# A two-layer hybrid decoder trunk on one core: another order of the DRAM round trips on GpSimd's queue

## The chip, the core and the metric

The kernel runs on one core of a Trainium2 chip. The metric is the device time of one execution in microseconds; where several runs are given, their median. The profile is one execution, recorded by the hardware profiler. Engine names are those of the profile: PE is TensorE's matrix multiply and PEld its weight load, DVE is VectorE, ACT is ScalarE, POOL is GpSimd, SP is SyncE. A DMA that GpSimd issues stands in GpSimd's own instruction queue, between its other instructions.

## What is computed

Two layers over 256 tokens of width 1024, batch 1, in float32. Each layer, shortened from the reference:

```python
h = rms_norm(x, norm_g[l])
q_a, k_a, v_a, q_h, f_h, i_h, q_m, z = split(h @ w_in[l])      # 7 x 512 columns, and 1536 for the gate z
o_a = moba_attention(rope(rms_norm(q_a)), rope(rms_norm(k_a)), v_a)   # 8 heads of 64, causal over the one block
o_h = rms_norm(hgrn2_chunkwise(q_h, f_h, i_h, lb[l]), o_norm)         # 4 heads of 128, gated linear recurrence
k_m, v_m = split(rms_norm(mem, mem_norm_g[l]) @ w_mem_kv[l])
o_m = memory_attention(rms_norm(q_m), rms_norm(k_m), v_m)             # 4 heads of 128 over 256 memory tokens
y = concatenate([o_a, o_h, o_m]) * silu(z)
x = x + y @ w_out[l]
```

With 256 tokens and blocks of 256 keys there is no fully past block, so the block-sparse attention reduces to causal attention.

## The kernel before

**Weights.** Every weight passes through in chunks of 512 KB: `wr` is the chunk as loaded by SyncE's queue (4 buffers), `wh` its rounded high part, cast on ScalarE (lines 186 and 189; 3 buffers), `wl` the rest, formed on VectorE (lines 198 and 201; 3 buffers). A product takes three matmul passes, high by high, high by low and low by high, into four PSUM accumulators `acc`. Chunks are loaded up to five ahead, `wh` up to three and `wl` up to two ahead of TensorE.

**Order of one layer.** Memory keys and values; the projections f_h, q_h, k_a, i_h, q_a, the gate of the recurrent group (`zh`), q_m, v_a; then the gates of the other two groups, eight chunks c0 to c7 of the kind `acc<-hT,wh` and `acc<-hT,wl`; then `w_out`, twelve chunks (line 1164), which start with the four of the recurrent group. Of each gate chunk the low half of the accumulator is copied out by ScalarE (`al`, line 323) and added by VectorE (`as`, line 324).

**Side work.** Around this main row of matmuls run generators, small programs that yield between their pieces: `g_hgrn` (the recurrence), `g_moba` with two units `g_moba_unit` (four heads each), `g_mem_unit` and so on. A generator's piece is written into the program between two main matmul groups, and the framework's scheduler then places each instruction on its engine from a simulated timeline and the dependences. On an engine, instructions run strictly in the order so placed.

**The round trips.** `across` (lines 88 to 110) turns a tile over partitions and columns: VectorE transposes 32x32 blocks into `blk`, one DMA stores `blk` to a DRAM tile `there`, and four DMAs load it back, each of them a quarter of the destination, 32 partitions. The four loads need the store's landing. Keys use SyncE's queue; three trips per layer use GpSimd's:

- the softmax P of unit 0 of the first group, to `PT` (768 KB)
- the P of unit 1, to `PT` (768 KB)
- the recurrent group's gated output `zh` (512 KB, line 754, `y_turned`). After it ScalarE casts it to `yh` (line 125, two instructions) and VectorE forms `yl` (line 126); these are the left-hand sides of the first four chunks of `w_out`.

Between them on GpSimd stand the small powers `hgr` and `qmr` (line 600) and `nrm` (line 1059), which the memory group's exponentials need. In `y_turned`, the generator waits, while the program is written, until unit 1's P has been transposed (`turned1`).

**What stands around w_out.** Between the first `w_out` matmuls stand the `PT` matmuls of the two units (line 244 and 240, `sd<-PT,va`) and the memory group's (`sd<-mP,vmh`); before them, in chunk c6, the transposes of the memory group's softmax (line 1128, `sd<-ident,P`).

Of the kernel before, what the change touches and what calls it, by code (L numbers as in the profile page):

```python
# [3 lines left out]

# [41 lines left out]
def hymba_kernel(ctx: ExitStack, tc: tile.TileContext, x, mem, mem_t, positions, w_in, w_out, w_mem_kv,  # L46
                 gains, moba_g, out):
    nc = tc.nc
# [15 lines left out]
    def room(what, n=1):  # L64
        while held[what] + n > room_of[what]:
            yield

    def take(*whats):
        for w in whats:
            yield from room(w)  # L70
        while any(held[w] >= room_of[w] for w in whats):
            yield
        for w in whats:
            held[w] += 1

    def side_tile():
        held["sd"] += 1
        assert held["sd"] <= 4
        return psum.tile([128, 512], F32, name="sd", tag="sd", bufs=4)

    def rel(what="sd", n=1):
        held[what] -= n

    def small(name, n):
        return sb.tile([128, n], F32, name=name, tag=name, bufs=2)


    def across(dst, src, n, stage=None, free=None, name=None, q=None):
        q = q or nc.sync
        if stage is None:  # L90
            yield from room("blk")
            held["blk"] += 1
        tag = stage or "blk"
        blk = sb.tile([128, 4, n * 32], F32, name="blk", tag=tag, bufs=1)
        nc.vector.transpose(blk.rearrange("p c (n i) -> p c n i", n=n),
                            src.rearrange("p (n c i) -> p c n i", n=n, c=4))
        if free is not None:
            rel(free)
        if name is not None:
            done.add(name)  # L100
        yield 2
        there = away.tile([4, 32, 4, n * 32], F32, name="there", tag="there", bufs=2)
        q.dma_start(there.rearrange("q j c r -> (q j) c r"), blk)
        if stage is None:
            rel("blk")
        yield 4
        for c in range(4):
            q.dma_start(dst[c * 32:c * 32 + 32], there[:, :, c].rearrange("q j r -> j q r"))  # L108
            if c == 1:
                yield  # L110

    def turned(a, stage=None, q=None):
        yield from across(a.rearrange("p (q r) -> p q r", q=4), a, 8, stage, q=q)
        yield 5

    def strips(a):
# [5 lines left out]
    def unstripped(oh, ol, a):  # L122
        for t in range(2):
            src, to = strips(a)[:, :, t], strip_of(oh, t)
            nc.scalar.copy(to, src)  # L125
            nc.vector.tensor_tensor(strip_of(ol, t), src, to.bitcast(F32), op=OP.subtract)
# [82 lines left out]
    done = set()  # L209
    T = {}  # L210
# [28 lines left out]
    def mm(o, a, b, s, e):  # L239
        nc.tensor.matmul(o, lhsT=a, rhs=b, start=s, stop=e)  # L240
# [337 lines left out]
    zh = sb.tile([128, 2, 512], F32, name="zh")  # L578
# [24 lines left out]
    def g_km(l, acc):  # L603
# [25 lines left out]
        kml = kt.bitcast(F32R)  # L629
        g = gkq[:, l:l + 1]  # L630
        yield from across(kt.rearrange("p (q r) -> p q r", q=4), kn.rearrange("p t s -> p (t s)"), 8)
        while f"ih{l}" not in done:
            yield
# [103 lines left out]
    def y_tiles(br):  # L737
        if f"y{br}" not in T:
            T[f"y{br}"] = [sb.tile([128, 4, 256], F32R, name=f"y{c}{br}", tag=f"y{c}{br}", bufs=1) for c in "hl"]
        return T[f"y{br}"]  # L740

    def y_store(l, br, u, po):
        yh, yl = (a.rearrange("p k s -> p (k s)")[:, u * 512:(u + 1) * 512] for a in y_tiles(br))
        ys = sb.tile([128, 512], F32, name="ys", tag="sq", bufs=2)
        nc.vector.tensor_tensor(ys, po, zT[br][:, u * 512:(u + 1) * 512], op=OP.mult)
        nc.scalar.copy(yh, ys)
        nc.vector.tensor_tensor(yl, ys, yh.bitcast(F32), op=OP.subtract)
        rel()
        for k in (2 * u, 2 * u + 1):
            done.add(f"y{4 * br + k}_{l}")  # L750

    def y_turned(l):
        flat = zh.rearrange("p t s -> p (t s)")
        while f"turned1{l}" not in done:
            yield
        yield from turned(flat, "hq0", nc.gpsimd)
        unstripped(*y_tiles(H_), flat)
        yield
        for k in range(4):
            done.add(f"y{4 * H_ + k}_{l}")  # L760

    def g_hgrn(l):
# [121 lines left out]
        for t in range(2):  # L884
# [5 lines left out]
            rel()  # L890
            yield
        yield from y_turned(l)


    def g_qk(l, q, acc):
# [37 lines left out]
        if q == 0:  # L933
            o = o.rearrange("p (h s) -> p h s", h=4)
            for t in range(2):
                yield from room("sd")
                pt = side_tile()
                for p in range(4):
                    nc.tensor.transpose(pt[:, p * 128:(p + 1) * 128], kr[:, t, p * 128:(p + 1) * 128], ident)  # L939
                nc.scalar.copy(o[:, :, t * 128:(t + 1) * 128], heads(pt, 4))  # L940
                rel()
                yield
        else:
            yield from across(o.rearrange("p (q r) -> p q r", q=4), flat, 8)
            yield 5
# [13 lines left out]
    def second(u):  # L959
        qT, kT = T["qT"], T["kT"]  # L960
        ps = [side_tile() for _ in range(2)]
        for pi in range(2):
            for e in range(2):
                mm_row(ps[e][:, pi * 256:(pi + 1) * 256].rearrange("p (t q i) -> p t q i", t=2, q=4),
                       qT[64 * e:64 * e + 64, 2 * u + pi, 128:256], strips(kT)[64 * e:64 * e + 64, 2 * u + pi])
        return ps

    def second_masked(u, ps, P, mx):
        for i in range(4):
            pi, e = divmod(i, 2)  # L970
            masked(P, i, 1, ps[e][:, pi * 256:(pi + 1) * 256], mx)
        rel("sd", 2)

    def g_moba_unit(l, u, P, mx):
        rq, nr = T["rq"], T["nr"]
        nb = small("nba%d" % u, 8)
        sm = small("sma%d" % u, 8)
        ri = small("ria%d" % u, 8)
        if u:
            yield from room("sd", 2)  # L980
            ps = second(u)
            yield
            second_masked(u, ps, P, mx)
        nc.vector.tensor_tensor(nb.rearrange("p (t h) -> p t h", t=2), mx.rearrange("p (t h) -> p t h", t=2),  # L984
                                nr.rearrange("p (t h) -> p t h", t=2)[:, :, 4 * u:4 * u + 4], op=OP.mult)
        yield
        for t in range(2):
            for i in range(4):
                c, r = t * 4 + i, t * 8 + 4 * u + i
                nc.scalar.activation(P[:, i, kc[t]], P[:, i, kc[t]], AF.Exp, bias=nb[:, c:c + 1],  # L990
                                     scale=rq[:, r:r + 1], accum_out=sm[:, c:c + 1])
            yield
        yield
        nc.vector.reciprocal(ri, sm)
        for t in range(2):
            for i in range(4):
                c = t * 4 + i
                nc.vector.tensor_scalar(P[:, i, kc[t]], P[:, i, kc[t]], ri[:, c:c + 1], None, op0=OP.mult)
        yield 2
        tag = ("PTh", "PTl")[u]  # L1000
        yield from take(tag)
        PT = sb.tile([128, 4, 384], F32, name="PT", tag=tag, bufs=1)
        yield from across(PT, P.rearrange("p i s -> p (i s)"), 12, free="P", name=f"turned{u}{l}", q=nc.gpsimd)
        yield 13
        while f"va{l}" not in done or f"z{A_}{l}" not in done:
            yield
        va = T["va"]
        yield from room("sd")
        po = side_tile()
        for i in range(4):  # L1010
            h = 4 * u + i
            rows, c = slice(64 * (i % 2), 64 * (i % 2) + 64), (i // 2) * 256
            pieces = PT.rearrange("p q (n s) -> p n q s", n=12)[:, 3 * i:3 * i + 3]
            o = po[rows, c:c + 256].rearrange("p (b q s) -> p b q s", b=2, q=4)
            (mm if i else mm_row)(o, va[:, 0, h * 64:(h + 1) * 64], pieces[:, 0:2], True, False)
            mm(o[:, 1], va[:, 1, h * 64:(h + 1) * 64], pieces[:, 2], False, True)
        rel(tag)
        yield
        y_store(l, A_, u, po)
# [258 lines left out]
```

## Time and profile before

| | us |
|---|---|
| median of three runs (396.27 to 397.12) | 396.33 |
| the profiled execution | 399.69 |
| its span, first to last instruction | 397.9 |
| PE busy | 390.5 |
| DVE busy | 314.6 |
| ACT busy | 251.1 |
| POOL busy | 70.3 |

The sums of the prediction are made against the profiled execution. Its span is 1.8 us shorter than its own time, and its time is 3.36 us above the median of the runs. Times in the profile's rows count from the span's start. A row of the timeline gives start, duration, engine, line, operation and shape; x4 means four instructions merged; the brackets say how long the engine had been idle before and what ended the idle time. A PE row's duration holds the time in the pipeline; in an undisturbed row of 128x512 matmuls one starts every 0.23 us or so. Layer 0's and layer 1's instructions are the same but for a few set-up steps.

### The profile page before, as it was taken

To read this page: it belongs to the slowest core of one execution; us is meant where nothing else is said; L and a number is where in the kernel's file an instruction comes from. 1 tells how busy PE (TensorE), PEld (TensorE's weight loads), DVE (VectorE), ACT (ScalarE), POOL (GpSimd) and SP (SyncE) were. 2 spreads that over 40 slices of the span, in tenths; PEclk is the share of its full clock that TensorE was granted. 3 is DMA by queue.
4 is the path that set the end of the run, shared out by engine and by line. 5 is a ranking of instruction groups with operands and counts; after the bars stand their busy time and mean duration, and the time that the engine had idled before them with its cause. 6 is when DMAs were issued, how large, how long until landed. Compare 5 with 4: busy or idle time off the path is not lost.

```text
span 397.9 us, 7596 instructions
## 1 busy us (share of the span) xinstructions
PE 390.5 (98%) x2871; PEld 326.1 (82%) x2871; DVE 314.6 (79%) x606; ACT 251.1 (63%) x422; POOL 70.3 (18%) x109
## 2 busy tenths in 40 slices
PE   8999999999999999999999999999999999979996
PEld 5888888878788888788888888887888789867885
DVE  4789999889759998964576889799965999766743
ACT  5998746557778669544466766546856884954440
POOL 2013401604103432000000040050330061400000
PEclk9999999999999999999999999999999999999999
DMA  8986794377634989546565469637943398981612
GB/s 267 411 294 213 245 244 158 100 259 218 202 110 152 238 308 263 205 122 219 188 202 169 164 215 238 234 107 226 249 163 107 105 281 271 270 236 55 203 61 105
DMA packets 24901, 80.33 MB, mean 202 GB/s; under 512 B 3233, under 2 KB 5665, under 8 KB 24865
## 3 DMA queue, kind: packets, MB, share of 16 engines
q1 hardware_dynamic: 22304, 71.31, 56.0%
q0 software_dynamic: 2272, 8.39, 7.9%
q8 instruction: 22, 0.36, 0.4%
q10 hardware_dynamic: 288, 0.15, 0.1%
q14 instruction: 15, 0.11, 0.1%
HBM read 72.51 MB, written 7.34 MB: 201 GB/s over the span
## 4 chain that ended last, share of the span: by engine, by line
PE 86%; DMA 4%; DVE 4%; POOL 2%; issue 2%; ACT 1%; SPq 0%; ACTq 0%; DVEq 0%; POOLq 0%
PE acc L240 58%; PE acc L1164 17%; PE sd L240 5%; PE sd L244 3%; DMA zh<-there 3%; DMA wr<-in_w_mem_kv_dram 1%; DVE wl L198 1%; PE sd L453 1%; ACT wh L186 1%; POOL rka L904 1%; POOL PT L108 0%; PE sd L1068 0%; PE sd L939 0%; PE sd L1128 0%; POOL rtB L548 0%
## 5 line engine op out<-in xcount | busy, mean ns | idle before, releaser
L198 DVE TENSOR_TENSOR wl<-wr,wh 128x1024 fp32r<-128x1024 f32 x96 | 116.8, 1219 | 39.4 <-ACT wh L186 39.3
L186 ACT CAST wh<-wr 128x1024 fp32r<-128x1024 f32 x96 | 100.6, 1050 | 67.0 <-PE acc L240 45.2
L240 PE MATMUL acc<-wh,hT 128*128 128x512 f32 x384 | 124.8, 396 | 0.0
L240 PEld LDWEIGHTS acc<-wh,hT 128*128 128x128 f32 x384 | 71.8, 188 | 16.1 <-issue 0.7
L240 PE MATMUL acc<-wl,hT 128*128 128x512 f32 x192 | 75.2, 392 | 0.0
L240 PE MATMUL acc<-hT,wh 128*128 128x512 f32 x256 | 65.2, 393 | 0.0
L240 PEld LDWEIGHTS acc<-hT,wh 128*128 128x128 f32 x256 | 45.9, 189 | 8.2 <-ACT kn L607 0.4
L240 PEld LDWEIGHTS acc<-wl,hT 128*128 128x128 f32 x192 | 36.1, 188 | 7.0 <-DVE wl L198 0.2
L201 DVE SCALAR_TENSOR_TENSOR wl<-wr,gT,wh 128x1024 fp32r<-128x1024 f32 (+1 forms) x29 | 31.2, 1097 | 12.4 <-ACT wh L189 12.1
L189 ACT ACTIVATE wh<-wr,gT 128x1024 fp32r<-128x1024 f32 (+1 forms) x29 | 28.6, 1002 | 16.5 <-PE acc L1164 8.2
L1164 PE MATMUL acc<-wl,yh 128*128 128x512 f32 (+1 forms) x96 | 37.7, 392 | 0.0
L240 PEld LDWEIGHTS acc<-hT,wl 128*128 128x128 f32 x256 | 35.2, 190 | 2.5
L1164 PE MATMUL acc<-wh,yl 128*128 128x512 f32 (+1 forms) x96 | 37.1, 392 | 0.0
L240 PE MATMUL acc<-hT,wl 128*128 128x256 f32 x256 | 36.6, 283 | 0.0
L1164 PE MATMUL acc<-wh,yh 128*128 128x512 f32 (+1 forms) x96 | 30.4, 396 | 2.0 <-ACT yh L125 2.0
L240 PE MATMUL acc<-wh,mTh 128*128 128x512 f32 x64 | 25.1, 395 | 0.5 <-DVE mTh L392 0.3
L240 PE MATMUL acc<-wh,mTl 128*128 128x512 f32 x64 | 24.8, 390 | 0.0
L1164 PEld LDWEIGHTS acc<-wh,yh 128*128 128x128 f32 x96 | 18.3, 190 | 6.1 <-ACT yh L125 2.2
L990 ACT ACTIVATE P<-P,nba,rq 128x128 f32<-128x128 f32 (+1 forms) x32 | 17.1, 535 | 8.3 <-DVE nba L984 8.3
L1164 PEld LDWEIGHTS acc<-wh,yl 128*128 128x128 f32 x96 | 18.3, 191 | 3.8
L1164 PEld LDWEIGHTS acc<-wl,yh 128*128 128x128 f32 x96 | 18.3, 191 | 3.6
L240 PE MATMUL acc<-wl,mTh 128*128 128x512 f32 x64 | 20.2, 392 | 0.0
(222 smaller groups left out, 575.0 us busy)
## 6 DMA issues: line engine op xcount, KB each, us to landing
wr<-in_w_in_dram SPq DMA_DIRECT2D x80, 512.0 KB, 4.2
wr<-in_w_out_dram SPq DMA_DIRECT2D x24, 512.0 KB, 5.1
wr<-in_w_mem_kv_dram SPq DMA_DIRECT2D x15, 512.0 KB, 4.4
there<-blk POOLq DMA_DIRECT2D x4, 768.0 KB, 4.2
PT<-there POOLq DMA_DIRECT2D x16, 192.0 KB, 6.9
there<-blk SPq DMA_DIRECT2D x4, 512.0 KB, 3.6
xs<-in_x_dram SPq DMA_DIRECT2D x2, 512.0 KB, 8.8
memr<-in_mem_dram SPq DMA_DIRECT2D x2, 512.0 KB, 6.7
```

Source lines behind the costliest of these rows:

```text
L186: nc.scalar.copy(whs[i], raws[i])
L189: nc.scalar.activation(whs[i][:, sl], raws[i][:, sl], AF.Copy, scale=gT[:, g:g + 1])
L198: nc.vector.tensor_tensor(wls[i], raws[i], whs[i].bitcast(F32), op=OP.subtract)
L201: ins = nc.vector.scalar_tensor_tensor(wls[i][:, sl], in0=raws[i][:, sl], scalar=gT[:, g:g + 1], in1=whs[i][:, sl].bitcast(F32), op0=OP.mu ...
L240: nc.tensor.matmul(o, lhsT=a, rhs=b, start=s, stop=e)
L244: tc.keep_in_program_order(nc.tensor.matmul(o, lhsT=a, rhs=b, start=s, stop=e))
L453: ins = nc.tensor.transpose(pt[:, j * 256 + t * 128:j * 256 + (t + 1) * 128], xn[t][:, k * 128:(k + 1) * 128], ident)
L904: nc.gpsimd.tensor_tensor(r[:, t8], ms[:, t8], pw[:, :8], op=OP.pow)
L990: nc.scalar.activation(P[:, i, kc[t]], P[:, i, kc[t]], AF.Exp, bias=nb[:, c:c + 1], scale=rq[:, r:r + 1], accum_out=sm[:, c:c + 1])
L1164: ins = nc.tensor.matmul(a, lhsT=y, rhs=wt[:, cs], start=n == (0 if to is None else nk - 2) and j == 0, stop=n == nk - 1 and j == 2)
```

## The change

`across` gets a parameter `behind`: the store to DRAM is then written into the program only once the trip of that name has issued its loads, and the scheduler is told to keep it behind the last of them. `y_turned` waits for the loads of unit 0's P to be issued (`turned0...moved`) and no longer for unit 1's transpose, and names its own trip `zh0` or `zh1`. Unit 1's P gets `behind` that name. The quarters of every trip, those on SyncE's queue too, are loaded in the order 0, 2, 1, 3. Behind unit 1's trip the generator yields once and not 13 times, since it has waited already.

```diff
-    def across(dst, src, n, stage=None, free=None, name=None, q=None):
+    def across(dst, src, n, stage=None, free=None, name=None, q=None, behind=None):
...
         yield 2
+        while behind is not None and behind not in done:
+            yield
         there = away.tile([4, 32, 4, n * 32], F32, name="there", tag="there", bufs=2)
-        q.dma_start(there.rearrange("q j c r -> (q j) c r"), blk)
+        with tc.issue_after(T[behind].ins) if behind is not None else nullcontext():
+            q.dma_start(there.rearrange("q j c r -> (q j) c r"), blk)
         if stage is None:
             rel("blk")
         yield 4
-        for c in range(4):
-            q.dma_start(dst[c * 32:c * 32 + 32], there[:, :, c].rearrange("q j r -> j q r"))
-            if c == 1:
+        for c in (0, 2, 1, 3):
+            ins = q.dma_start(dst[c * 32:c * 32 + 32], there[:, :, c].rearrange("q j r -> j q r"))
+            if c == 2:
                 yield
-
-    def turned(a, stage=None, q=None):
-        yield from across(a.rearrange("p (q r) -> p q r", q=4), a, 8, stage, q=q)
+        if name is not None:
+            T[name + "moved"] = ins
+            done.add(name + "moved")
+
+    def turned(a, stage=None, q=None, name=None):
+        yield from across(a.rearrange("p (q r) -> p q r", q=4), a, 8, stage, q=q, name=name)
         yield 5
...
-        while f"turned1{l}" not in done:
+        while f"turned0{l}moved" not in done:
             yield
-        yield from turned(flat, "hq0", nc.gpsimd)
+        yield from turned(flat, "hq0", nc.gpsimd, f"zh{l}")
...
-        yield from across(PT, P.rearrange("p i s -> p (i s)"), 12, free="P", name=f"turned{u}{l}", q=nc.gpsimd)
-        yield 13
+        yield from across(PT, P.rearrange("p i s -> p (i s)"), 12, free="P", name=f"turned{u}{l}", q=nc.gpsimd,
+                          behind=f"zh{l}moved" if u else None)
+        yield (13, 1)[u]
```

Line numbers of the changed kernel are 3 to 7 higher from `across` on. Where the instructions stand on three engines in layer 1 (layer 0 moves in the same way):

GpSimd's queue, from unit 0's loads on; `there<-blk 128x1536` is a store of P, `there<-blk 128x1024` the store of zh. Before:

```order
L108 DMA PT<-there 32x4x384 x4
L600 TENSOR_TENSOR qmr<-qmm,pw 128x8
L1059 TENSOR_SCALAR nrm<-qmr 128x8
L103 DMA there<-blk 128x1536
L103 DMA there<-blk 128x1024
L108 DMA PT<-there 32x4x384 x4
L108 DMA zh<-there 32x4x256 x4
```

and now:

```order
L111 DMA PT<-there 32x4x384 x4
L606 TENSOR_TENSOR qmr<-qmm,pw 128x8
L106 DMA there<-blk 128x1024
L1066 TENSOR_SCALAR nrm<-qmr 128x8
L111 DMA zh<-there 32x4x256 x4
L106 DMA there<-blk 128x1536
L111 DMA PT<-there 32x4x384 x4
```

zh's store went from behind the second P's store to behind `qmr`, and its four loads from the end of the row to ahead of that store.

ScalarE's queue, in the gate chunks, from the cast of c5's `wh` to the cast of c7's; the ACTIVATE P rows are the memory group's exponentials. Before:

```order
L186 CAST wh<-wr 128x1024
L323 COPY al<-acc 128x256
L186 CAST wh<-wr 128x1024
L1107 ACTIVATE P,smm_3828<-sd,nbm_3827,qmr 128x256 x4
L323 COPY al<-acc 128x256
L1107 ACTIVATE P,smm_3888<-sd,nbm_3887,qmr 128x256 x4
L731 ACT_TABLE_LOAD
L731 ACTIVATE sg<-as 128x512
L186 CAST wh<-wr 128x1024
```

and now:

```order
L192 CAST wh<-wr 128x1024
L131 CAST yh_4142<-zh 128x4x128 x2
L329 COPY al<-acc 128x256
L192 CAST wh<-wr 128x1024
L1114 ACTIVATE P,smm_3826<-sd,nbm_3825,qmr 128x256 x4
L329 COPY al<-acc 128x256
L1114 ACTIVATE P,smm_3882<-sd,nbm_3881,qmr 128x256 x4
L737 ACT_TABLE_LOAD
L737 ACTIVATE sg<-as 128x512
L192 CAST wh<-wr 128x1024
```

The two `yh` casts, which stood behind the memory group's last `mP` cast, now stand ahead of the exponentials, with the wait for zh's loads on the first of them. On VectorE the two `yl` moved likewise, to ahead of c6's `wl`.

TensorE, at the end of the gate chunks; `acc<-hT,wl ... x8` is the end of c7. Before, the `PT` matmuls of unit 0 follow, of which the first rows stand here:

```order
L240 MATMUL acc<-hT,wh 128x512 x8
L240 MATMUL acc<-hT,wl 128x256 x8
L244 MATMUL sd<-PT,va 64x256
L240 MATMUL sd<-PT,va 64x128
```

and now:

```order
L246 MATMUL acc<-hT,wh 128x512 x8
L246 MATMUL acc<-hT,wl 128x256 x8
L1171 MATMUL acc<-wh,yh_4142 128x512
L1171 MATMUL acc<-wl,yh_4142 128x512
L1171 MATMUL acc<-wh,yl_4143 128x512
L1171 MATMUL acc<-wh,yh_4142 128x512 x2
L1171 MATMUL acc<-wl,yh_4142 128x512
```

Twelve `w_out` matmuls now stand between c7 and the side work, where before six stood between the memory group's first matmuls and unit 1's `PT` matmuls. The transposes of the memory group's softmax moved some matmuls later inside c6.

More of the change, by code (lines that the diff above doesn't have):

```diff
@@ L1 @@
 import math
-from contextlib import ExitStack
+from contextlib import ExitStack, nullcontext
 from fractions import Fraction
```

## The prediction, made before the changed kernel ran

> **What bounds the kernel now.** I read the page first, then the chain that ended last, then the stretch in which that chain leaves TensorE.
>
> ```profile
> PE 390.5 (98%) x2871; PEld 326.1 (82%) x2871; DVE 314.6 (79%) x606; ACT 251.1 (63%) x422; POOL 70.3 (18%) x109
> PE 86%; DMA 4%; DVE 4%; POOL 2%; issue 2%; ACT 1%; SPq 0%; ACTq 0%; DVEq 0%; POOLq 0%
> ```
>
> TensorE is busy nearly all the time, so the change can only win where TensorE waits or runs slowly, and it loses wherever it makes TensorE wait. The chain shows one such place, late in layer 1:
>
> ```profile
> 345.52 10.21 DMA zh<-there
> 355.84 0.63 ACT yh L125
> 356.51 2.93 PE acc L1164 x6
> ```
>
> The fourth quarter of zh is issued at 345.52 and lands 10.2 us later; ScalarE then splits zh into yh, and the first six matmuls of w_out follow. I set this stretch beside the same one of layer 0 (timeline of TensorE; from the first PT matmul of unit 0 to the first matmul behind unit 1's):
>
> ```profile
> 351.30 0.43 PE L244 MATMUL sd<-PT,va 128*64 128x256 f32 x1
> 354.22 0.28 PE L240 MATMUL sd<-mP,vmh 128*128 128x256 f32 x1
> 356.51 0.79 PE L1164 MATMUL acc<-wh,yh 128*128 128x512 f32 x1 [2.01 <-ACT yh L125]
> 361.08 0.51 PE L1164 MATMUL acc<-wh,yh 128*128 128x512 f32 x1
> 159.28 0.43 PE L244 MATMUL sd<-PT,va 128*64 128x256 f32 x1
> 165.75 0.51 PE L1164 MATMUL acc<-wh,yh 128*128 128x512 f32 x1
> ```
>
> It takes 361.08 - 351.30 = 9.78 us in layer 1 and 165.75 - 159.28 = 6.47 in layer 0, for the same work. The 3.31 us are the wait of 2.01 and a slow start behind it, which the windows show as a granted clock of 0.57 (columns: PE, PEld, DVE, ACT, POOL busy, clock, DMA share, GB/s):
>
> ```profile
> 352.00:356.00 4.00, 2.50 (x24) 2.08 (x20) 1.43 (x3) 0.16 (x1) 0.00 (x0) 1.00 0.98 333
> 356.00:360.00 4.00, 3.49 (x10) 2.27 (x12) 3.51 (x6) 3.69 (x7) 0.00 (x0) 0.57 0.08 34
> ```
>
> Layer 0 has no such wait, so the prize is layer 1's 3.3 us, and some 0.3 per layer of short waits (an estimate: the PT and mP blocks take 354.50 - 351.30 = 3.2, a second PT block half of that, six w_out matmuls 1.4; 6.2 against 6.47): 3.9 in all.
>
> **Part 1: zh's store ahead of the second P's.** GpSimd's queue in layer 1, and the DVE transpose of zh that its store waits for:
>
> ```profile
> 317.30 0.64 POOL L103 DMA_DIRECT2D there<-blk  x1 [25.43 <-DVE hgm L598]
> 321.88 2.24 POOL L108 DMA_DIRECT2D PT<-there  x4 [1.58 <-PE acc L240]
> 323.27 1.25 DVE L95 STREAM_TRANSPOSE blk<-zh 128x1024 f32<-128x1024 f32 x1
> 324.14 1.72 POOL L600 TENSOR_TENSOR qmr<-qmm,pw 128x8 f32<-128x8 f32 x1
> 333.03 1.20 POOL L103 DMA_DIRECT2D there<-blk  x2 [6.77 <-DVE blk L95]
> 338.11 2.25 POOL L108 DMA_DIRECT2D PT<-there  x4 [3.88 <-PE acc L240]
> 340.68 1.67 POOL L108 DMA_DIRECT2D zh<-there  x3 [0.31 <-issue]
> ```
>
> zh is transposed by 324.52, but its store stands behind the second P's and leaves near 333.7. Now it leaves when qmr ends, 325.9. nrm, behind it, comes some 0.6 later (one issue); what it feeds are the exponentials of part 2, far later, so that is free. How long the store takes there no row shows; the nearest are these (issue rows and times to landing):
>
> ```profile
> L103 POOL DMA_DIRECT2D there<-blk x1: 641/641/641, 317.3 to 317.3; - x1
> DMA to landing us min/median/max: 3.9/3.9/3.9
> L103 POOL DMA_DIRECT2D there<-blk x2: 551/598/645, 333.0 to 333.7; - x2
> DMA to landing us min/median/max: 4.3/5.3/6.3
> L108 POOL DMA_DIRECT2D PT<-there x1: 605/605/605, 321.9 to 321.9; - x1
> DMA to landing us min/median/max: 5.9/5.9/5.9
> L108 POOL DMA_DIRECT2D PT<-there x2: 550/550/550, 323.0 to 323.6; - x2
> DMA to landing us min/median/max: 6.7/6.8/6.9
> kT<-there SPq DMA_DIRECT2D x8, 128.0 KB, 4.9
> ```
>
> With nothing ahead: 3.9, landing at 329.8. Behind other work of the same queue: zh's store of before landed at 333.7 + 6.3 = 340.0, 2.7 after the P store ahead of it (333.0 + 4.3 = 337.3); the four PT quarters ahead of it now land last at 323.6 + 6.9 = 330.5, which gives 333.2. I take 331.5, the middle, because the DMA engines run full only to about 329:
>
> ```profile
> 324.00:328.00 4.00, 4.00 (x25) 3.57 (x25) 4.00 (x12) 2.45 (x5) 2.16 (x3) 1.00 1.01 234
> 328.00:332.00 4.00, 4.00 (x29) 3.71 (x28) 4.00 (x5) 1.32 (x3) 0.00 (x0) 1.00 0.73 240
> ```
>
> A load follows its store's landing by 0.7 (321.88 - 317.3 - 3.9), so the quarters go out from 332.2. From first issue to last landing the PT quarters of 192 KB took 330.5 - 321.9 = 8.6; quarters of zh's size, 128 KB, are kT's, with 4.9 for one, and three more issues of 0.55 make 6.6. I take 7.2, nearer to kT because the bytes are kT's. So zh is there at **339.4**, between 329.8 + 0.7 + 6.6 = 337.1 and 333.2 + 0.7 + 8.6 = 342.5, against 355.7 before. The wait at w_out goes: TensorE reaches w_out at 351.3 at the earliest, whichever end holds. That w_out's first twelve matmuls now stand ahead of PT and mP adds no work; it needs w_out's first weights earlier, which part 2 charges.
>
> **Part 2: where yh now stands on ScalarE.** The two casts stood at 355.84; now they stand right behind the wh cast at 334.75, and every later ScalarE instruction queues behind their wait. Layer 1, then layer 0:
>
> ```profile
> 334.75 1.05 ACT L186 CAST wh<-wr 128x1024 fp32r<-128x1024 f32 x1 [1.46 <-PE acc L240]
> 337.54 1.05 ACT L186 CAST wh<-wr 128x1024 fp32r<-128x1024 f32 x1 [1.47 <-PE acc L240]
> 338.50 0.56 ACT L1107 ACTIVATE P<-sd,nbm,qmr 128x256 f32<-128x256 f32 x1
> 345.09 1.03 ACT L186 CAST wh<-wr 128x1024 fp32r<-128x1024 f32 x1
> 348.45 1.98 PE L240 MATMUL acc<-hT,wh 128*128 128x512 f32 x8
> 355.84 1.14 ACT L125 CAST yh<-zh 128x512 fp32r<-128x512 f32 x2 [4.63 <-DMA zh<-there]
> 146.47 0.56 ACT L1107 ACTIVATE P<-sd,nbm,qmr 128x256 f32<-128x256 f32 x1
> 153.07 1.03 ACT L186 CAST wh<-wr 128x1024 fp32r<-128x1024 f32 x1
> 156.42 1.98 PE L240 MATMUL acc<-hT,wh 128*128 128x512 f32 x8
> ```
>
> ScalarE is free at 335.8 and waits to 339.4. Then yh (1.05), the al copy (0.25) and the wh cast (0.95) run, and the exponentials start at about 339.4 + 0.1 + 2.25 = 341.75 instead of 338.50: 3.25 late. From there to the cast at 345.09 ScalarE has no gap to absorb it. That cast is the hi half of the last gate chunk (c7): it ended at 346.12 and TensorE took it at 348.45, so 2.3 are covered and about 0.95 are not. The lo halves on VectorE, which also waits for yh before its next wl, and w_out's first weights I put at another 0.4 (an estimate: one to two matmuls of 0.23 for each of the two). Layer 0 shows the same distances, shifted by 192.02 (338.50 - 146.47, 348.45 - 156.42), so I charge it the same 1.35, with no wait of 2 us to win.
>
> **Part 3: the second P.** Its store was free to go at 333.03; now it waits for the last zh issue, about 334.4, and its quarters follow some 1.5 to 3 us later than 338.11. Unit 1's PT matmuls stand behind unit 0's, at about 357 to 359, so this is covered. The issues on GpSimd stay the same in number.
>
> **Part 4: quarters 0, 2, 1, 3.** Whoever reads needs all four, so only their common end counts. The window 324 to 328 shows the DMA engines at 1.01 with 234 GB/s while PT quarters fly, against 333 at 0.98 in 352 to 356: quarters cost DMA time. Bound: nothing to 1 us off the 8.6; I take nothing. The Trainium skill (SBUF — State Buffer, Can I just issue two DMAs to hit both halves?) says that partitions 0 to 63 reach the same 8 of 16 ports and that two transfers to different halves gain only 6%. By it this part would give about 0.2 us per group, and the trace's 234 agrees with a port limit.
>
> **Sum.** Won 3.9, lost 2 x 1.35 = 2.7: 1.2 us. The profiled execution would go from 399.69 to 398.5. The runs' median lies 3.36 below it; I carry that over, 396.33 - 1.2 = **395.1**. Each us by which zh comes later costs 2, one per layer. The end points: zh by 338.4 costs no stall, 3.9 won, 392.4; zh at 342.5 costs 2 x 4.45 = 8.9, a net loss of 5.0, 401.3. Break-even is zh at 340.0.
>
> **Rivals.** (A) The forecast, zh between 338.5 and 339.6. (B) zh early enough to hide in the 2.3 us of cover: for it speaks the DMA share of 0.73 when the store would run, against it that no group of quarters above was quicker than 6.6; 392.4 to 393.2. (C) The wait moves to ScalarE: zh lands past 340.5, because its store queues behind the first P's quarters and its quarters share the engines with weight loads. For it speak the 2.7 by which zh's store trailed the one ahead and the share of 1.01 up to 328; against it the share of 0.73 behind that. It decides from 340.4; at 341.3 it gives 2 x 3.25 - 3.9 = 2.6 lost, 398.9. The Trainium skill (DMA: Bandwidth & Descriptors, Queues, rings and completion order) has each DMA engine take one ring's descriptors in order. By that rule the store starts behind the PT quarters and the upper end is the likelier; no row here shows a store behind loads. (D) A wash, 395.5 to 397.1: zh near 340, or the runs do not have all of the 3.3 us. That the runs lie 3.36 us under the profiled execution speaks for a smaller prize; that ScalarE then waits less, too, speaks against a loss.
>
> **Chances.** A 0.38, B 0.14, C 0.28, D 0.20. A measurement here tells 0.2%, 0.8 us, from no change: faster A + B = 0.52, same 0.20, slower 0.28. A's own range is 393.3 to 395.5. Leaving out the tails of B and C gives 392.6 to 398.9.
>
> **What would show it.** Right: in GpSimd's timeline zh's store at about 325.9 and its quarters from 332; yh on ScalarE ahead of the exponentials with an idle of 3 to 4 us put down to the zh DMA; no wait for yh at w_out and clock 1.00 in layer 1; about 1 us of idle on TensorE before the last gate chunk in both layers. Wrong: an idle of 5 us or more before yh with TensorE waiting for wh or P (C), no idle there at all (B), or TensorE waiting for PT of unit 1 (part 3).

## The result: slower, 401.55 us against 396.56

The changed kernel took 401.55 us (median of four runs, 401.37 to 404.26), the kernel before, on the same chip, 396.56 (396.27 to 397.12): a ratio of 1.0148, 95% interval 1.0107 to 1.0188. The prediction was 395.1 with a range of 392.6 to 398.9, so sign and range are both missed.

The profiled execution is the one of 404.26 us, span 402.2. Two further executions of the changed kernel stand on record beside the four, at 404.05 and 402.14. Engines and chain on the page of the changed kernel:

```profile
PE 392.1 (97%) x2871; PEld 326.6 (81%) x2871; DVE 315.3 (78%) x606; ACT 250.8 (62%) x422; POOL 71.4 (18%) x109
PE 79%; ACT 5%; DVE 5%; DMA 4%; POOL 3%; issue 2%; SPq 0%; ACTq 0%; DVEq 0%
```

Before, TensorE held 86% of the chain and ScalarE 1%; now ScalarE has 5%. Its pieces, in layer 1 (the chain in order of time: start, length, what):

```profile
346.62 0.62 ACT yh L131
347.50 0.95 ACT wh L192
348.45 2.14 ACT P L1114 x8
350.78 2.32 ACT P L1114 x8
353.12 1.28 ACT L737
354.95 1.04 ACT wh L192
```

These are yh, c6's `wh`, the two groups of exponentials, the table load and c7's `wh`, one after another, with only short pieces of ScalarE's own between them (the `al` copies, the `sg` of line 737): the queue of part 2. GpSimd's timeline of the changed kernel, layer 0, then layer 1:

```profile
132.26 2.24 POOL L111 DMA_DIRECT2D PT<-there  x4 [1.54 <-PE acc L246]
136.62 0.60 POOL L106 DMA_DIRECT2D there<-blk  x1
143.36 2.23 POOL L111 DMA_DIRECT2D zh<-there  x4 [5.75 <-DMA there<-blk]
327.17 2.24 POOL L111 DMA_DIRECT2D PT<-there  x4 [1.56 <-PE acc L246]
331.05 0.61 POOL L106 DMA_DIRECT2D there<-blk  x1
339.12 2.23 POOL L111 DMA_DIRECT2D zh<-there  x4 [6.84 <-DMA there<-blk]
```

ScalarE's, yh and c7's `wh` in both layers:

```profile
151.32 1.14 ACT L131 CAST yh<-zh 128x512 fp32r<-128x512 f32 x2 [5.20 <-DMA zh<-there]
160.18 1.03 ACT L192 CAST wh<-wr 128x1024 fp32r<-128x1024 f32 x1
346.09 1.14 ACT L131 CAST yh<-zh 128x512 fp32r<-128x512 f32 x2 [4.98 <-DMA zh<-there]
354.95 1.03 ACT L192 CAST wh<-wr 128x1024 fp32r<-128x1024 f32 x1
```

And TensorE's idle times in the same place (the memory group's transposes, then c7's first matmuls):

```profile
161.26 2.15 PE L246 MATMUL acc<-hT,wh 128*128 128x512 f32 x8 [0.60 <-ACT wh L192]
351.77 0.41 PE L1135 MATMUL sd<-ident,P 128*128 128x128 f32 x2 [0.46 <-DVE P L1125]
353.85 0.41 PE L1135 MATMUL sd<-ident,P 128*128 128x128 f32 x2 [0.54 <-DVE P L1125]
356.04 2.11 PE L246 MATMUL acc<-hT,wh 128*128 128x512 f32 x8 [0.47 <-ACT wh L192]
```

The wait at `w_out` is gone. What came in its place is one wait of 5 us on ScalarE per layer, of which TensorE feels a part. Its three idle times in layer 1 sum to 1.47 us: two are put down to VectorE's `P`, which is made from ScalarE's exponentials, and one to ScalarE's `wh`. They are not the whole delay. From c6's first matmul to c7's it takes 356.04 - 349.19 = 6.85 us, against 348.67 - 344.11 = 4.56 in e1 below, 2.3 more; the rest lies in gaps between the matmuls that are too short to be listed.

To compare the two profiles stage by stage I count from the issue of unit 0's P loads, which the change does not touch. In layer 0 of the kernel before it stood here:

```profile
129.94 2.24 POOL L108 DMA_DIRECT2D PT<-there  x4 [1.56 <-PE acc L240]
```

So the changed kernel's profile runs 2.32 us late at that point, and 5.29 in layer 1 (327.17 - 321.88). The first 2.3 come from the start of this execution. TensorE, changed kernel:

```profile
7.54 0.80 PE L246 MATMUL acc<-wh,mTh 128*128 128x512 f32 x1 [1.23 <-ACT wh L195]
11.05 0.39 PE L246 MATMUL acc<-wh,mTh 128*128 128x512 f32 x1
```

and before:

```profile
6.22 0.50 PE L240 MATMUL acc<-wh,mTh 128*128 128x512 f32 x1
8.55 0.50 PE L240 MATMUL acc<-wh,mTh 128*128 128x512 f32 x1 [0.22 <-ACT wh L189]
```

The second group of eight matmuls starts 11.05 - 8.55 = 2.50 later: TensorE waited 1.23 us for a weight cast, and behind that wait the windows show a granted clock of 0.50 (8 to 10 us), so that the matmuls between took 11.05 - 7.54 = 3.51 us and not 8.55 - 6.22 = 2.33. It is not the change's: the same kernel with another order of quarters (e6 below) has its first P loads at 130.45. The three other runs of the four, at 401.37 to 401.60, fit a start without it. The rest of the loss lies between the P loads of layer 0 and the end:

| profile | layer 0's P loads to layer 1's | layer 1's to the span's end |
|---|---|---|
| before | 191.94 | 76.02 |
| before, second profile (e7) | 192.48 | 72.16 |
| changed | 194.91 | 75.03 |
| changed, quarters in order (e6) | 194.75 | 74.70 |
| changed, yh late (e1) | 191.96 | 72.24 |

Against e1 the change costs 2.95 us in layer 0 and 2.79 in layer 1; against the second profile of before 2.43 and 2.87. Only the first profile of before hides the loss in layer 1, since its own layer 1 is 3.8 us longer than that of the second.

### The profile page after: what moved, and what is told of

Same layout as the page of the kernel before. It is cut to its first block, busy times and chain, and to the rows that moved or that the text cites. A ratio compares the mean times of both kernels' runs of the same rounds, so it can differ in the third digit from the quotient of the medians.

```text
span 402.2 us, 7610 instructions
## 1 busy us (share of the span) xinstructions
PE 392.1 (97%) x2871; PEld 326.6 (81%) x2871; DVE 315.3 (78%) x606; ACT 250.8 (62%) x422; POOL 71.4 (18%) x109
## 4 chain that ended last, share of the span: by engine, by line
PE 79%; ACT 5%; DVE 5%; DMA 4%; POOL 3%; issue 2%; SPq 0%; ACTq 0%; DVEq 0%
PE acc L246 53%; PE acc L1171 16%; PE sd L246 5%; PE sd L250 4%; ACT P L1114 2%; DMA there<-blk 2%; DMA zh<-there 2%; ACT wh L192 2%; DMA wr<-in_w_mem_kv_dram 1%; DVE wl L204 1%; PE sd L459 1%; ACT L737 1%; DVE wl L207 1%; POOL PT L111 1%; POOL qmr L606 1%
```

## The experiments

**e1: yh behind the exponentials.** The main theory (1): ScalarE's queue, held by yh. The rival (2): the new DMA order disturbs the weight loads.

```diff
     yield from turned(flat, "hq0", nc.gpsimd, f"zh{l}")
-    unstripped(*y_tiles(H_), flat)
+    while f"exps{l}" not in done:
+        yield
+    with tc.issue_after(T["exp"].ins):
+        unstripped(*y_tiles(H_), flat)
```

> The changed kernel with one thing undone: the two yh casts and yl may be placed only behind the memory group's last exponential; GpSimd's queue and the quarter order stay changed. Theory 1 (the loss is the wait for zh at the head of ScalarE's and VectorE's queues, ahead of the exponentials and of c7's wh): that wait goes, 395.5 to 397.0. Theory 2 (the loss is the DMA traffic: zh's trip ahead of the second P holds up weights and PT wherever yh stands): stays at 400.5 to 402.

Measured: 396.26 us, ratio 0.9973 of the kernel before (0.9948 to 0.9997). GpSimd's order and its DMAs are the changed kernel's; only the two casts (and yl) moved. The chain by engine, GpSimd's loads and ScalarE's timeline in layer 1:

```profile
PE 90%; DVE 4%; DMA 2%; POOL 1%; ACT 1%; issue 1%; SPq 0%; ACTq 0%; DVEq 0%
333.19 2.23 POOL L111 DMA_DIRECT2D zh<-there  x4 [6.16 <-DMA there<-blk]
338.73 0.56 ACT L1117 ACTIVATE P<-sd,nbm,qmr 128x256 f32<-128x256 f32 x1
345.33 1.03 ACT L192 CAST wh<-wr 128x1024 fp32r<-128x1024 f32 x1
346.26 1.14 ACT L131 CAST yh<-zh 128x512 fp32r<-128x512 f32 x2
```

The store still lands late (6.16 of waiting), the exponentials start at once, and yh at 346.26 waits for nothing. The whole loss is gone with yh moved back on ScalarE and yl on VectorE: theory 1 holds, theory 2 falls. What yl's place alone is worth no run tells.

**e2: the changed kernel without the wait.** zh's four loads go to a tile `spare` that nobody reads, and yh is made from zh as it was before the turn; the turning of zh is left out.

```diff
-    yield from turned(flat, "hq0", nc.gpsimd, f"zh{l}")
+    spare = sb.tile([128, 1024], F32, name="spare", tag="spare", bufs=1)
+    yield from across(spare.rearrange("p (q r) -> p q r", q=4), flat, 8, "hq0", q=nc.gpsimd, name=f"zh{l}")
+    yield 5
```

> The changed kernel with the same store and loads of zh on GpSimd, but the loads go to a spare tile and yh is cast from zh as it was before the trip, so the turning of zh is left out of the result and nothing waits for its loads. Theory 1: 395.5 to 396.8. Theory 2: 400 or more, since the traffic is the same.

Measured: 396.29 us, 0.9978 (0.9954 to 1.0002). All DMAs are issued as in the changed kernel:

```profile
333.53 2.23 POOL L111 DMA_DIRECT2D spare<-there  x4 [5.94 <-DMA there<-blk]
```

The transfers without a reader cost nothing that this measurement tells, so the loss is the wait and not the traffic.

**e3: the kernel before without the wait.** The same `spare` in the kernel before, the turning of zh left out. It measures the prize: what the best possible placement could win.

> The kernel before with zh's loads into a spare tile and yh cast from the unturned zh (the turning is left out of the result), so w_out waits for no load of zh. It measures the prize. If the 3.3 us that the profile of before shows in layer 1 are in the timed runs too: 392.7 to 393.5. If they belong to the profiled execution alone: 395.8 to 396.6, equal to before.

Measured: 396.22 us against 396.62 of the kernel before beside it, 0.9967 (0.9936 to 0.9999). The medians lie 0.4 us apart; the ratio says 1.3 us, with an interval from nothing to 2.5. The profile that I predicted from promised 3.9.

**e4: the order of the quarters alone,** in the kernel before.

```diff
-        for c in range(4):
+        for c in (0, 2, 1, 3):
             q.dma_start(dst[c * 32:c * 32 + 32], there[:, :, c].rearrange("q j r -> j q r"))
-            if c == 1:
+            if c == 2:
```

> The kernel before with the loads of every trip in the order 0, 2, 1, 3 and nothing else. The prediction took nothing for it: 396.0 to 396.9. If the two port halves can be loaded side by side, the third and fourth quarter land earlier and it is at most 1 us faster, 395.3; theory 1 and theory 2 say the same here, no loss.

Measured: 396.50 us, 0.9979 (0.9954 to 1.0004): no difference that this measurement tells. The Trainium skill (SBUF — State Buffer, Can I just issue two DMAs to hit both halves?) says that transfers to the two halves of the partitions serialize; the result does not contradict it, but the 0.2 us that the prediction worked out lies inside the interval. Its profile again shows a wait at `w_out` in layer 1, of another length than the first:

```profile
355.81 0.50 PE L1164 MATMUL acc<-wh,yh 128*128 128x512 f32 x1 [1.35 <-ACT yh L125]
```

**e5: zh's store on SyncE's queue.** The second question: why did the store land 6.4 and 7.7 us after its issue (the DMA rows of the two layers), and not 5.6?

```diff
-            q.dma_start(there.rearrange("q j c r -> (q j) c r"), blk)
+            (nc.sync if stage == "hq0" else q).dma_start(there.rearrange("q j c r -> (q j) c r"), blk)
```

> The changed kernel, only that zh's store is issued by SyncE's queue; its four loads stay on GpSimd's. Nothing is left out. It asks why zh landed late: the store left when it was due but took 6.5 and 7.4 us to land (issue of the store to the end of what the loads waited for), against 3.9 for the first P's store with nothing ahead of it. Theory 1 (one queue is served in order: the store's descriptors stand behind those of the four PT quarters): on another queue it lands about 4 to 4.5 us after its issue, zh is there some 2 to 3 us earlier, the wait of ScalarE ahead of yh falls from 5.0-5.2 to 2.5-3 us, and the time from 401.4 to 396.5-398.5 us. Theory 2 (the DMA engines are simply full while the quarters fly, whatever the queue): it lands 6 us or more after its issue as before, and the time stays at 400.5 to 402 us. A possible disturbance: SyncE's queue carries the weight loads, and the store may be held behind those; then it leaves late and lands late, which the issue row would show.

Measured: 400.65 us, 1.0096 (1.0058 to 1.0134). The issue rows of store and loads:

```profile
134.48 0.33 SPq L106 DMA_DIRECT2D there<-blk  x1
142.64 2.26 POOL L111 DMA_DIRECT2D zh<-there  x4 [7.49 <-DVE blk L95]
327.72 0.33 SPq L106 DMA_DIRECT2D there<-blk  x1
334.26 2.26 POOL L111 DMA_DIRECT2D zh<-there  x4 [4.77 <-DVE wl L204]
```

From the store's issue to the loads' it is 8.2 and 6.5 us, against 6.7 and 8.1 in the changed kernel; the DMA rows give 7.6 and 5.8 us to its landing, against 6.4 and 7.7. So the other queue was later in layer 0 and sooner in layer 1, which is no clear gain. The time is in theory 2's range, and so is the landing in layer 0; the 5.8 of layer 1 is just under the 6 us written down. It is no clean test, because SyncE's queue holds weight loads of its own, and because the wait for the loads in layer 1 is put down to VectorE and not to the store. The Trainium skill (DMA: Bandwidth & Descriptors, Issuing engines are not separate DMA queues) says that all queues run on the same 16 DMA engines and interleave there; the rows agree with it and do not prove it.

**e6: the changed kernel with quarters 0, 1, 2, 3.** The edit is e4's, undone.

> The changed kernel with its quarters loaded in the order 0, 1, 2, 3 again, nothing else undone. If the order of the quarters has no part in the loss (as with the kernel before, where the order 0, 2, 1, 3 alone gave 0.9979 of its time, interval 0.9954 to 1.0004): 401.0 to 402.0 us, ScalarE's wait ahead of yh 4.8 to 5.4 us in both layers. Rival: the order 0, 2, 1, 3 slows each group of loads, and with it zh's landing, by half a microsecond or more: then at most 400.5 us and a wait shorter by 0.5 us or more. Or it helped: 402.5 us or more.

Measured: 402.26 us, 1.0146 (1.0092 to 1.0200), beside 1.0148 for the changed kernel. ScalarE's waits ahead of yh:

```profile
149.27 1.14 ACT L131 CAST yh<-zh 128x512 fp32r<-128x512 f32 x2 [4.64 <-DMA zh<-there]
343.70 1.14 ACT L131 CAST yh<-zh 128x512 fp32r<-128x512 f32 x2 [4.61 <-DMA zh<-there]
```

The waits are 0.4 to 0.6 shorter than with 0, 2, 1, 3, a little below what I had written down, and the time does not follow: it lies 0.26 above the range written down for no part in the loss. The order of the quarters has no measurable part in the result.

**e6b: zh ahead of the first P's quarters.** The four loads of unit 0's P are put behind zh's loads, so that no PT quarter flies when the store leaves.

```diff
+        while late is not None and late not in done:
+            yield
         for c in (0, 2, 1, 3):
-            ins = q.dma_start(dst[c * 32:c * 32 + 32], there[:, :, c].rearrange("q j r -> j q r"))
+            with tc.issue_after(T[late].ins) if late is not None else nullcontext():
+                ins = q.dma_start(dst[c * 32:c * 32 + 32], there[:, :, c].rearrange("q j r -> j q r"))
...
-        while f"turned0{l}moved" not in done:
+        while f"turned0{l}stored" not in done:
...
-                          behind=f"zh{l}moved" if u else None)
+                          behind=f"turned0{l}moved" if u else None, late=None if u else f"zh{l}moved")
```

> The changed kernel, with the four loads of unit 0's P put behind zh's loads on GpSimd's queue; the order of ScalarE stays that of the changed kernel, with yh ahead of the exponentials. Nothing is left out. zh's store then leaves with no PT quarter in flight. The run with the store on SyncE's queue left open whether those quarters or the weight loads on SyncE's own queue delayed it. Theory 1 (the PT quarters ahead of it made the store late): from its issue to the issue of zh's loads 4.5 to 5.2 us instead of 6.7 and 8.1, zh there 2 to 3 us earlier, ScalarE's wait ahead of yh 2 to 3 us instead of 5.0 to 5.2, hardly any idle of TensorE before c7's first matmul, and 396.0 to 397.3 us: the same order on ScalarE costs nothing once zh is there by 338.5 on the clock of the profile before. Theory 2 (the weight loads fill the DMA engines whether the quarters fly or not): 6 us or more again, a wait of 4.5 us or more, and 400.5 to 402 us. A rival to both: the first P's quarters now come late and TensorE waits for PT at w_out; then the time is above 397.3 with no wait for wh or P.

Measured: 399.7 us (397.62 to 402.61), 1.0057 (1.0027 to 1.0086). GpSimd, ScalarE and TensorE:

```profile
134.37 0.64 POOL L106 DMA_DIRECT2D there<-blk  x1 [2.82 <-DVE lbs L687]
139.33 2.22 POOL L117 DMA_DIRECT2D zh<-there  x4 [4.32 <-DMA there<-blk]
331.20 0.64 POOL L106 DMA_DIRECT2D there<-blk  x1 [1.70 <-DVE blk L95]
335.56 2.23 POOL L117 DMA_DIRECT2D zh<-there  x4 [3.72 <-ACT wh L198]
148.34 1.14 ACT L137 CAST yh<-zh 128x512 fp32r<-128x512 f32 x2 [4.46 <-DMA zh<-there]
343.72 1.14 ACT L137 CAST yh<-zh 128x512 fp32r<-128x512 f32 x2 [4.16 <-DMA zh<-there]
166.82 0.40 PE L256 MATMUL sd<-PT,va 128*64 128x256 f32 x1 [2.34 <-DMA PT<-there]
```

The time lies between the ranges of the two theories. For the store, theory 1 came true: from its issue to the loads' it is now 5.0 and 4.4 us, and it landed after 4.7 and 3.7, against 6.4 and 7.7 (DMA rows). With PT's quarters issued right behind them, zh's loads took 148.34 - 139.33 = 9.0 and 343.72 - 335.56 = 8.2 us to yh's start, against 8.0 and 7.0 in the changed kernel, so the quarters gave a part back. Counted from the issue of the first P's store (125.35 and 323.57 here, 127.59 and 322.61 in the changed kernel), yh starts 0.74 us earlier in layer 0 and 3.33 in layer 1.

In layer 1 that was enough:

```profile
323.57 0.65 POOL L106 DMA_DIRECT2D there<-blk  x1 [25.43 <-DVE hgm L610]
353.53 1.03 ACT L198 CAST wh<-wr 128x1024 fp32r<-128x1024 f32 x1
354.71 2.00 PE L252 MATMUL acc<-hT,wh 128*128 128x512 f32 x8
```

Counted from that store, against the profile of before, c7's `wh` cast is (353.53 - 323.57) - (345.09 - 317.30) = 2.17 late and c7's first matmul is not late at all (31.14 against 31.15); TensorE waits for nothing there. The order on ScalarE did not quite stay: in layer 1 yh stands one `wh` cast earlier than in the changed kernel. So an early yh cost TensorE nothing where it started by 337.45 on the prediction's clock (343.72 - 323.57 + 317.30), as theory 1 said. The loss of this run is in layer 0, where yh is still late, c7's first matmul comes 1.78 late, and TensorE waits 2.34 us for PT, with a granted clock of 0.63 behind it (168 to 172 us). That is not quite the rival as written: by the chain the wait ends with the load issued at 160.00, the last quarter of the second P and not of the first. The second P's loads left at 158.33, 6.4 us later than in the changed kernel (154.20), both counted from the first P's store. This execution is the longest of the ten, so the size of that wait need not be that of the others. The quarters ahead, then, delay the store's loads by 1.8 and 3.7 us; whether in the queue or on the DMA engines stays open, since e5 does not decide it.

**e7: the kernel before once more.**

> The kernel before once more, unchanged, for a second profile of it. If the 3.3 us of layer 1 (the wait of 2.01 us for yh and the slow matmuls behind it) belong to the one profiled execution: the stretch from the first PT matmul of unit 0 to the first matmul behind unit 1's takes about 6.5 us in both layers, the span is 395 us or less, and the time is 396.0 to 396.8 us. If they belong to the kernel: about 9.8 us in layer 1 again, a span of about 398 us.

Measured: 396.38 us, 0.9995 (0.9970 to 1.0019); the profiled execution took 397.01, span 395.2. TensorE, from the first PT matmul of unit 0 to the first matmul behind unit 1's, in both layers:

```profile
159.92 0.43 PE L244 MATMUL sd<-PT,va 128*64 128x256 f32 x1
163.37 0.50 PE L1164 MATMUL acc<-wh,yh 128*128 128x512 f32 x1 [0.26 <-ACT yh L125]
166.91 0.51 PE L1164 MATMUL acc<-wh,yh 128*128 128x512 f32 x1
352.41 0.43 PE L244 MATMUL sd<-PT,va 128*64 128x256 f32 x1
355.45 0.40 PE L1164 MATMUL acc<-wh,yh 128*128 128x512 f32 x1
358.43 0.51 PE L1164 MATMUL acc<-wh,yh 128*128 128x512 f32 x1
```

6.99 us in layer 0 and 6.02 in layer 1, with a wait for yh of 0.26 in layer 0 and none in layer 1. So the 9.78 of the first profile is no property of every execution. It need not be the only one of its kind: among the 31 runs of the kernel before that stand beside e1, three (399.04 to 400.72 us) have the first profile's granted clock of 0.995, and among the 41 runs of e1, e2, e3 and e8 none is above 397.09 us or under a clock of 0.998. That fits a wait that costs some 3 us in about one execution of ten (an estimate from these counts) and that e1's order takes away; as none of those three runs has a profile, it is not shown.

**e8: e1's kernel in more rounds.**

> The kernel of e1_yh_late once more (the changed kernel with the yh casts behind the memory group's exponentials), in more rounds. Nothing is left out. If it beats the kernel before by what leaving zh's wait out altogether gained (0.2 to 0.3%): a ratio of 0.9965 to 0.998 with an interval that ends under 1. If that gain was chance: 0.999 to 1.001.

Measured: 396.34 us, 0.9986 (0.9976 to 0.9995). The gain is real but about half of what I expected: 0.14%, some 0.6 us. It is the version that beats both kernels.

## Why the prediction was wrong, step by step

**The prize (section Sum) failed first.** The 3.3 us of layer 1 were read rightly from the profile, but most executions do not have them. Three profiles of the order before show a wait for yh in layer 1 of 2.01, 1.35 (e4) and 0 (e7). The profiled execution lay 3.36 us above the median of the runs, nearly the same number, and I carried the gap over to the new kernel (399.69 to 398.5, 396.33 to 395.1) instead of asking whether the gap was the prize. It was, in the main: leaving the wait out won 0.4 us by medians (e3), and e8's kernel 0.6. So the term of 3.9 measured 0.4 to 0.6 by medians, and 2.5 at the most by e3's interval. Rival D named this possibility, as a wash.

**Part 1, zh's landing, was 1.3 to 1.4 us too early.** Counted from the P loads, and set on the prediction's clock (321.88 for layer 1's):

| step | predicted | layer 0 | layer 1 |
|---|---|---|---|
| store issued | 325.9 | 326.24 | 325.76 |
| loads issued | 332.2 | 332.98 | 333.83 |
| yh starts | 339.5 | 340.94 | 340.80 |
| c7's `wh` cast, late by | 3.25 | 4.79 | 4.57 |
| c7's first matmul, late by | 0.95 | 2.52 | 2.30 |

The store left when I said. The middle value of 331.5 for its landing was the mis-sized term in layer 1; the upper end from the neighbouring rows, 333.2, gives loads at 333.9 and was met (333.83). In layer 0 half of the excess is the loads' own 8.0 against 7.2. My argument for the middle, that the DMA engines run full only to about 329, did not hold. In the changed kernel they stay nearly full while the store flies; its window from 328.7 to 332.7 on the prediction's clock shows a share of 0.97, where before had 0.73 from 328 to 332:

```profile
334.00:338.00 4.00, 4.00 (x31) 3.78 (x30) 4.00 (x5) 0.71 (x2) 0.00 (x0) 1.00 0.97 336
```

That the upper end was met does not show why: for the descriptors' order in one ring, which the prediction named beside it, e5 is the nearest test, and there the store landed later in one layer and sooner in the other.

**Part 2, the mechanism, was right, and its size followed part 1.** The cover of c7's cast was put at 2.3: measured 4.79 - 2.52 and 4.57 - 2.30, both 2.27. The further 0.4 fits: 2.95 and 2.79 lost in all (against e1), 0.43 and 0.49 more than c7's delay; but against e7's profile it would be -0.09 and 0.57, and no run splits it between VectorE and w_out's weights, so a part of that match may be luck. In layer 1 of e6b a cast 2.17 late made no matmul late, so the cover is shown from both sides. With zh 1.4 later, the prediction's own price, 1.35 + 1.4 = 2.75 per layer, gives 5.5 for two layers; less the 0.4 of e3 it makes 5.1, and 401.55 - 396.56 = 4.99 was measured, closer than this measurement can tell. Break-even at 340.0 rested on the prize; with a prize of 0.4 there was none to reach at any landing that I held likely, since 339.4 already lost 2.7.

**Part 3 was right in its verdict:** no wait for unit 1's PT in the changed kernel, though its quarters left at 349.12 - 5.29 = 343.83, 5.7 later than before and not 1.5 to 3. In layer 0 of e6b, with those quarters another 6.4 later, the cover is used up.

**Part 4 was right:** e4 and e6.

**The rivals.** What happened is C (zh past 340.4, the wait moved to ScalarE, with its sign: 5.20 and 4.98 us of idle before yh and TensorE waiting for `P` and `wh`) together with the second half of D. I priced C with the prize still won, which gave 398.9, and gave it 0.28. Each us of delay was priced twice, once per layer, but the gain was in one layer only; that asymmetry, and a landing time good to no better than 2 us either way, spoke against the sign that I chose.

## What to carry to other kernels

When an early transfer lets a consumer be placed earlier, look first at what stands behind that consumer on its engine: an instruction that waits for a DMA holds up everything written after it, and here two casts of 1.14 us together cost 2.9 us per layer until they stood behind the work that was ready. Before a stall in one profile is counted as a prize, set the profiled execution against the median of the runs: if it is longer by about the size of the stall, the stall may be missing from most executions, and a second profile, or a run with the wait left out, tells. Where a loss grows with each us of a landing time that is bounded only to 3 or 5 us, price the whole band before choosing the sign.

## What the runs showed of the hardware that I had not expected

- A store of 512 KB on GpSimd's queue behind four loads of 192 KB: 6.7 and 8.1 us from its issue to that of the loads that need it; without those loads ahead, 5.0 and 4.4 (e6b). The store itself landed after 6.4 and 7.7 us, and after 4.7 and 3.7. The loads of zh, with PT's behind them, took 9.0 and 8.2 us, against 8.0 and 7.0 without.
- The eighth load in a row on GpSimd's queue was held. In e7, after four loads of PT and three of zh:

```profile
343.17 1.68 POOL L108 DMA_DIRECT2D zh<-there  x3
347.79 0.55 POOL L108 DMA_DIRECT2D zh<-there  x1 [2.95 <-issue]
```

In e6b, with four of zh and three of PT ahead, the eighth was held likewise, 1.94 us in layer 0 and 0.37 in layer 1, until a load of zh had landed. The kernel before meets this in each layer, on the last quarter of zh; in the changed kernel no eight loads stand together. No run here tells what the limit is made of.

- TensorE's granted clock fell behind some waits: to 0.57 (356 to 360 us) behind 2.01 us in the profile of before, to 0.50 (8 to 10 us) behind 1.23 at the start of the changed kernel's, to 0.63 (168 to 172 us) behind 2.34 in e6b. Behind the 1.35 of e4 it stayed at 1.00 (356 to 360 us). The matmuls behind the first three ran slower, so such a wait cost more than its length; no run here tells what decides it.
